# Dense expert stage: the next four experts' first activation is traced between the second and third block's values instead of in front of all five

## The chip, the cores and the metric

The kernel runs on one core of one Trainium2 chip. The metric is the device time of one execution in microseconds (us). Five engines of the core run instruction streams of their own: PE (matmuls), DVE (elementwise), ACT (activations and casts), POOL (here: it issues the indirect loads of single rows) and SP (it issues all other loads). Each engine takes its stream strictly in order; semaphores tie them together.

## The reference, cut to what matters

The reference is one layer of a streaming encoder over 1024 prompt and 128 sample tokens: attention and an RG-LRU, then a PEER layer, in which each token has 8 heads that choose 16 of 16384 one-neuron experts each. The change lies in the PEER layer:

```
act = jax.nn.gelu(jnp.einsum('thkd,td->thk', expert_u[e_idx], xt))
out = jnp.einsum('thk,thkd->td', g * act, expert_v[e_idx])
```

The 1152 tokens are nine blocks of 128. Four blocks (`GATHER`) load the rows of their experts one by one. The other five (`DENSE`, 640 tokens) are computed against all 16384 experts: with a matrix G of weights that is zero wherever a token has not chosen an expert, out = (G * gelu(U x)) V. The experts come as 128 groups of 128; the kernel calls such a group an expert, `e`.

## The kernel before

`dense` works through the 128 groups in 32 chunks of `ECH = 4`. In one chunk there are two kinds of work.

`u_phase(e, gt)`, once for each of four groups: load 512 KB of `peer_ut` into a `raw` buffer, split it into a high and a low part (`hi` on ACT, L141; `lo` on DVE, L142), and multiply in two halves of 320 tokens, 24 matmuls each (three products for each of 8 slices, L175 to L177), into two `pp` buffers in PSUM. ACT takes the gelu of each half into `wf` (L1043; this tile has a single buffer). DVE multiplies `wf` by that group's slice of `gt` (L1045), and the product is split into `wh` (ACT, L141) and `wl` (DVE, L142). The next group's gelu can't be written until `wl` has been read out of `wf`.

`v_phase(c, ws, vs)`, once for each chunk: for each of the five token blocks, in the order 2, 0, 3, 1, 4, it accumulates four groups times three products times two halves, so 24 matmuls of 512 columns (L1069), into an `S` buffer in PSUM. Blocks 0 and 1 keep buffers of their own over the whole stage. Blocks 2, 3 and 4 take turns in the one remaining buffer: each must be added into its `acc` by DVE (L1077) before the next may start.

`load_v(e)` loads 512 KB of `peer_v` into a `raw` buffer and splits it (`vh`, `vl`; four buffers each, free when the last block of a chunk has read them). The pool `raw` has four buffers, shared by the loads of both kinds. `load_g(c)` loads the four slices of G for a chunk (`gt`, 1280 KB, L1056) into a single buffer, so it can't be issued until the last group of the chunk before has been multiplied at L1045.

The loop before traces, for chunk c: `u_phase` and `load_v` of groups 1, 2, 3; `load_g` of the next chunk; `u_phase` of the next chunk's group 0; `v_phase`; `load_v` of the next chunk's group 0. The work of the five blocks therefore stands behind the first activation of the next chunk.

After the dense stage the code traces `gather` for the blocks 5, 6 and 7, and what the earlier stages have left of block 0: for each row a load issued by POOL into one of six buffers (L910, 512 KB) and a DVE instruction of 1.2 to 1.3 us (L937 for the dot products, L958 for the sums).

The order on each engine is not the order of the code. The program is built under `tile.TileContext(nc, schedule_with_timeline_sim=True)`: a planner lays out each engine's stream before the run, by the durations that it assumes. What is traced first has priority; what is traced later is put in where the planner sees an engine free and the operands ready. In this way DVE carries rows of the gather between the instructions of the dense stage, and PE takes matmuls of `v_phase` between those of `u_phase`. On the chip the streams are fixed: an instruction whose operand is late holds up everything behind it on its engine.

Of the kernel before, what the change touches and what calls it, by code (L numbers as in the profile page):

```python
# [58 lines left out]
ECH = 4  # L59
AT_ONCE = (0, 5)  # L60
LAG = 3
FLOW = ((0,) * 5, (0.2, 0.26, 0.26, 0.26, 0.26), (0.13, 0.26, 0.3, 0.26, 0.26))


def r32(ap):
    return ap.bitcast(F32R)
# [3 lines left out]
def kernel(ctx, tc, a):  # L70
# [49 lines left out]
    def rstd_of(ss, q_="", r=None):  # L120
        m = sm_p.tile([128, 1], F32, name="rs_m" + q_)
        V.tensor_scalar(m, ss, 1.0 / D, EPS, op0=ALU.mult, op1=ALU.add)
        if r is None:
            r = sm_p.tile([128, 1], F32, name="rs_r" + q_)
        S.activation(r, m, ACTF.Sqrt)
        V.reciprocal(r, r)
        q = sm_p.tile([128, 1], F32, name="rs_q" + q_)
        V.tensor_tensor(q, r, r, op=ALU.mult)
        V.tensor_tensor(q, q, m, op=ALU.mult)
        V.tensor_scalar(q, q, -0.5, 1.5, op0=ALU.mult, op1=ALU.add)  # L130
        V.tensor_tensor(r, r, q, op=ALU.mult)
        return r

    def ssq(x, junk, q_=""):
        ss = sm_p.tile([128, 1], F32, name="ss" + q_)
        S.activation(junk, x, ACTF.Square, accum_out=ss)  # L136
        return ss
# [13 lines left out]
    def load_split(src, hi=None, lo=None, shape=(128, KT, 128), raw=None, key=None):  # L151
        if raw is None:
            raw = w_p.tile(list(shape), F32, name="raw", tag="raw", bufs=RAW_BUFS)
            nc.sync.dma_start(raw, src)
        if hi is None and phase[0] in THIRD and nw[0] % 3 == 2:
            hi = g_p.tile(list(shape), F32, name="hi", tag="g3")
            lo = g_p.tile(list(shape), F32, name="lo", tag="g4")
        elif hi is None:
            hi = w_p.tile(list(shape), F32, name="hi", tag="hi")
            lo = w_p.tile(list(shape), F32, name="lo", tag="lo")  # L160
        nw[0] += 1
        if key in lo_d:
            S.copy(r32(hi), raw)  # L163
            nc.sync.dma_start(lo, lo_d[key])
            return hi, lo
        split(hi, lo, raw)
        if phase[0] == 0 and key:

            lo_d[key] = dr_p.tile(list(shape), F32, name="lo_%s%d" % key)
            nc.sync.dma_start(lo_d[key], lo)  # L170
        return hi, lo

    def mm3(out, l, r, first, last):
        (lh, ll), (rh, rl) = l, r
        T.matmul(out, r32(lh), r32(rh), start=first, stop=False)  # L175
        T.matmul(out, r32(lh), r32(rl), start=False, stop=False)  # L176
        T.matmul(out, r32(ll), r32(rh), start=False, stop=last)  # L177
# [9 lines left out]
    def transpose_in(x, dst, c0, ps_s=ps_s):  # L187

        pt = ps_s.tile([128, 8, 128], F32, name="tr", tag="S")
        for k in range(8):  # L190
            T.transpose(pt[:, k, :], x[:, k * 128:(k + 1) * 128], ident)
        split(dst[:, 0, :, c0:c0 + 128], dst[:, 1, :, c0:c0 + 128], pt)
# [13 lines left out]
    def tick(n=1):  # L206

        for _ in range(n):
            if fill:
                fill.popleft()()  # L210
# [37 lines left out]
    def mixer(mp, gi, t0, xn):  # L248
# [20 lines left out]
        def beat(us):  # L269
# [9 lines left out]
            if flow:  # L279
                due[1] += FLOW[gi][stage[0]] * us  # L280
                while due[1] >= 1.0:
# [618 lines left out]
    def finish(b, x2, tmp, nf=None, q_=""):  # L900
        r = rstd_of(ssq(x2, tmp, q_), q_)
        if nf is None:
            nf = tmp
            nc.sync.dma_start(nf, a["norm_final"].to_broadcast([128, D]))
        V.scalar_tensor_tensor(x2, x2, r, nf, op0=ALU.mult, op1=ALU.mult)  # L905
        nc.sync.dma_start(a["y"][b], x2)
# [7 lines left out]
    def gather(b):  # L914
# [7 lines left out]
        nc.sync.dma_start(xt, xt_d[b])  # L922
        lag = LAG if early else 0

# [93 lines left out]
    def dense(dp):  # L1018
        nd = len(DENSE)
        Td = nd * 128  # L1020
        xt2 = dp["x"].tile([128, 2, KT, Td], F32, name="xd")
        accs = [None, None]
        for i, b in enumerate(DENSE):
            x = (w_p.tile([128, D], F32, name="xt", tag="raw", bufs=RAW_BUFS) if i < RAW_BUFS else
                 w_p.tile([128, D], F32, name="xt", tag="lo"))
            nc.sync.dma_start(x, xt_d[b])
            transpose_in(x, xt2, i * 128, dp["ps"])

        ps_p = dp["pp"]
        ps_s = dp["ps"]  # L1030

        def u_phase(e, gt):
            tick(2)
            hi, lo = load_split(a["peer_ut"][e], raw=u0 if e == 0 else None)
            wh = dp["w"].tile([128, Td], F32, name="wh")
            wl = dp["w"].tile([128, Td], F32, name="wl")
            w = dp["w"].tile([128, Td], F32, name="wf", bufs=1)
            for m in range(0, Td, Td // 2):
                c1 = slice(m, m + Td // 2)
                ps = ps_p.tile([128, Td // 2], F32, name="pp", tag="pp")  # L1040
                for k in range(KT):
                    mm3(ps, (hi[:, k, :], lo[:, k, :]), (xt2[:, 0, k, c1], xt2[:, 1, k, c1]), k == 0, k == KT - 1)
                S.activation(w[:, c1], ps, ACTF.Gelu_apprx_tanh)  # L1043
            w3 = w.rearrange("p (c t) -> p c t", t=32)
            V.tensor_tensor(w3, w3, gt[:, :, e % ECH, :], op=ALU.mult)  # L1045
            split(wh, wl, w)
            return wh, wl

        def load_v(e):
            vh = dp["v"].tile([128, D], F32, name="vh")  # L1050
            vl = dp["v"].tile([128, D], F32, name="vl")
            return load_split(a["peer_v"][e], vh, vl, (128, D))

        def load_g(c):
            gt = dp["g"].tile([128, NCH, ECH, 32], F32, name="gt")
            nc.sync.dma_start(gt, G_d[:, :, c * ECH:(c + 1) * ECH, :].rearrange("n p i t -> p n i t"))  # L1056
            return gt

        kept = [ps_s.tile([128, 2, 512], F32, name="S", tag="S") for _ in range(2)]

        def v_phase(c, ws, vs, nf=None):
            for i in (2, 0, 3, 1, 4):
                held = i < len(kept)
                po = kept[i] if held else ps_s.tile([128, 2, 512], F32, name="S", tag="S")
                c1 = slice(i * 128, i * 128 + 128)
                for n, ((wh, wl), (vh, vl)) in enumerate(zip(ws, vs)):
                    for q, (l, r) in enumerate(((wh, vh), (wh, vl), (wl, vh))):
                        for m in range(2):
                            T.matmul(po[:, m, :], r32(l[:, c1]), r32(r[:, m * 512:m * 512 + 512]),  # L1069
                                     start=(n == 0 and q == 0 and (c == 0 or not held)),  # L1070
                                     stop=(n == ECH - 1 and q == 2 and (c == nch - 1 or not held)))
                if held and c == nch - 1:
                    acc = w_p.tile([128, D], F32, name="acc", tag="lo")
                    nc.sync.dma_start(acc, x2_d[DENSE[i]])
                    accs[i] = acc
                if not held or c == nch - 1:
                    V.tensor_tensor(accs[i], accs[i], po.rearrange("p m c -> p (m c)"), op=ALU.add)  # L1077
                if c == nch - 1:
                    finish(DENSE[i], accs[i], w_p.tile([128, D], F32, name="yo", tag="hi"), nf)

        nch = 128 // ECH
        gt = load_g(0)
        ws, vs = [u_phase(0, gt)], [load_v(0)]
        for i in range(2, nd):
            acc = dp["x"].tile([128, D], F32, name=f"acc{i}")
            nc.sync.dma_start(acc, x2_d[DENSE[i]])
            accs.append(acc)
        for c in range(nch):
            for e in range(c * ECH + 1, (c + 1) * ECH):
                ws.append(u_phase(e, gt))  # L1090
                vs.append(load_v(e))
            nxt = []
            if c + 1 < nch:
                gt = load_g(c + 1)
                nxt = [u_phase((c + 1) * ECH, gt)]
            nf = None
            if not nxt:
                nf = w_p.tile([128, D], F32, name="nf", tag="raw", bufs=RAW_BUFS)
                nc.sync.dma_start(nf, a["norm_final"].to_broadcast([128, D]))
            v_phase(c, ws, vs, nf)  # L1100
            ws = nxt
            vs = [load_v((c + 1) * ECH)] if nxt else []

    mp = {nm: es_m.enter_context(tc.tile_pool(name=nm, bufs=bufs, reuse_waits="tile"))
          for nm, bufs in (("big", 2), ("s", S_BUFS), ("kv", 2), ("b", 2), ("c", 4))}
# [39 lines left out]
    for n, blocks in enumerate(GROUPS):  # L1145
# [17 lines left out]
        for b in SELECT[n]:  # L1163
            if b in AT_ONCE:
                fill.extend(late_picks[b])
            else:
                _, rest, heads = select(b)
# [132 lines left out]
```

## Time and profile before

| what | us |
|---|---|
| time, median of three runs | 3982.32 (3981.56 to 3986.05) |
| the profiled execution | 3979.21 |
| its span, first to last instruction | 3977.3 |
| dense stage, first to last matmul of it | 2010.1 to 3966.5 |

The span is the time between the first and the last instruction in the trace. The profiled execution's own time lies 1.9 us above its span and 3.1 us below the median. All stretches below are in us from the start of the span.

### The profile page before, as it was taken

How to read it: one execution, taken by the hardware profiler on the slowest of the kernel's cores; microseconds unless marked ns; L12 is line 12 of the kernel's file. 1: busy time of each engine (PE TensorE's matmuls, PEld its weight loads, DVE VectorE, ACT ScalarE, POOL GpSimd, SP SyncE). 2: the span in 40 equal slices, each digit the busy share in tenths (PEclk: the TensorE clock that was granted, in tenths of full speed). 3: DMA queues.
4: the chain of work that ended last, by engine and by line, in shares of the span. 5: the costliest groups of instructions: out<-in, count | busy, mean ns of one | idle time of the engine just before them, and what ended most of it. 6: DMA issues, size and time to landing. Idle time of an engine off the chain costs nothing. (4 is left out here: it accounts for less than half of the span.)

```text
span 3977.3 us, 59539 instructions
## 1 busy us (share of the span) xinstructions
PE 3647.0 (92%) x21775; PEld 3264.7 (82%) x21775; DVE 3042.7 (77%) x6332; ACT 1618.2 (41%) x2699; POOL 1405.4 (35%) x1094
## 2 busy tenths in 40 slices
PE   8998899898998999888888889999999899999998
PEld 7877799876887987778888778888888888888887
DVE  8433357868675879987778888888877887877887
ACT  7554346556644845665532122222222222222222
POOL 0000000122221023222106555655664655655653
PEclk9999999999998999999999999999999999999999
DMA  7778887888899898879968888989888889888986
GB/s 260 253 243 317 296 283 271 327 308 269 316 385 331 294 346 292 292 281 360 379 203 308 306 287 296 320 314 343 311 305 293 322 313 332 311 304 305 331 311 233
DMA packets 470358, 1208.05 MB, mean 304 GB/s; under 512 B 41008, under 2 KB 199088, under 8 KB 467504
## 3 DMA queue, kind: packets, MB, share of 16 engines
q1 hardware_dynamic: 292496, 638.23, 45.2%
q0 software_dynamic: 147456, 536.94, 37.8%
q10 hardware_dynamic: 30112, 29.09, 2.1%
q8 instruction: 170, 2.79, 0.3%
q14 instruction: 124, 1.02, 0.1%
HBM read 1066.15 MB, written 137.94 MB: 303 GB/s over the span
## 5 line engine op out<-in xcount | busy, mean ns | idle before, releaser
L910 POOL DMA_INDIRECT row<-peer_u,ei x512 | 698.0, 1363 | 1260.5 <-DVE row L937 631.3
L910 POOL DMA_INDIRECT row<-peer_v,ei x512 | 683.3, 1334 | 828.7 <-DVE x L958 525.4
L958 DVE SCALAR_TENSOR_TENSOR x<-row,q,x 128x1024 f32<-128x1024 f32 x512 | 655.3, 1280 | 27.2 <-DMA row<-peer_v,ei 20.8
L175 PE MATMUL pp<-xd,hi 128*128 128x320 f32 x2048 | 639.8, 312 | 31.9 <-ACT wf L1043 26.9
L937 DVE SCALAR_TENSOR_TENSOR row<-row,xt 128x1024 f32<-128x1024 f32 x512 | 613.6, 1217 | 66.1 <-DMA row<-peer_u,ei 64.4
L176 PE MATMUL pp<-xd,hi 128*128 128x320 f32 x2048 | 637.5, 311 | 0.3 <-DVE xd L142 0.3
L177 PE MATMUL pp<-xd,lo 128*128 128x320 f32 x2048 | 636.8, 311 | 0.0
L175 PE MATMUL pp<-xn,hi 128*128 128x384 f32 x1344 | 477.4, 356 | 19.1 <-ACT st L1011 7.8
L1069 PE MATMUL S<-vh,wh 128*128 128x512 f32 x1280 | 410.0, 402 | 62.2 <-DVE acc L1077 54.0
L177 PE MATMUL pp<-xn,lo 128*128 128x384 f32 x1344 | 459.4, 343 | 2.1 <-DMA lo<-lo_w_in 2.1
L176 PE MATMUL pp<-xn,hi 128*128 128x384 f32 x1344 | 460.6, 343 | 0.1
L1069 PE MATMUL S<-vh,wl 128*128 128x512 f32 x1280 | 401.1, 402 | 27.6 <-DVE wl L142 27.6
L175 PEld LDWEIGHTS pp<-xd,hi 128*128 128x128 f32 x2048 | 389.9, 190 | 42.6 <-ACT wf L1043 30.7
L141 ACT CAST hi<-raw 128x1024 fp32r<-128x1024 f32 x223 | 233.8, 1049 | 429.0 <-PE pp L176 307.2
L1069 PE MATMUL S<-vl,wh 128*128 128x512 f32 x1280 | 404.0, 397 | 0.0
L176 PEld LDWEIGHTS pp<-xd,hi 128*128 128x128 f32 x2048 | 389.8, 190 | 7.2 <-DVE xd L142 0.6
L177 PEld LDWEIGHTS pp<-xd,lo 128*128 128x128 f32 x2048 | 389.2, 190 | 1.6
L142 DVE TENSOR_TENSOR lo<-raw,hi 128x1024 fp32r<-128x1024 f32 x223 | 271.9, 1220 | 150.1 <-ACT hi L141 134.8
L141 ACT CAST wh<-wf 128x640 fp32r<-128x640 f32 x128 | 93.3, 729 | 616.8 <-DVE wf L1045 583.6
L1069 PEld LDWEIGHTS S<-vh,wh 128*128 128x128 f32 x1280 | 239.3, 193 | 112.3 <-DVE acc L1077 60.9
L163 ACT CAST hi<-raw 128x1024 fp32r<-128x1024 f32 x192 | 200.4, 1047 | 296.5 <-PE pp L176 204.3
L1069 PEld LDWEIGHTS S<-vh,wl 128*128 128x128 f32 x1280 | 246.7, 194 | 84.6 <-DVE wl L142 32.7
(296 smaller groups left out, 6821.7 us busy)
## 6 DMA issues: line engine op xcount, KB each, us to landing
raw<-w_in SPq DMA_DIRECT2D x168, 512.0 KB
raw<-peer_v SPq DMA_DIRECT2D x128, 512.0 KB
raw<-peer_ut SPq DMA_DIRECT2D x127, 512.0 KB
lo<-lo_w_in SPq DMA_DIRECT2D x112, 512.0 KB
G_d<-st SPq DMA_DIRECT2D x20, 2048.0 KB
gt<-G_d SPq DMA_DIRECT2D x32, 1280.0 KB
lo_w_in<-lo SPq DMA_DIRECT2D x56, 512.0 KB
raw<-wq SPq DMA_DIRECT2D x48, 512.0 KB
```

Of the source, the lines that this page charges most:

```text
L141: S.copy(r32(hi), src)
L142: ins = V.tensor_tensor(r32(lo), src, hi, op=ALU.subtract)
L163: S.copy(r32(hi), raw)
L175: T.matmul(out, r32(lh), r32(rh), start=first, stop=False)
L176: T.matmul(out, r32(lh), r32(rl), start=False, stop=False)
L177: T.matmul(out, r32(ll), r32(rh), start=False, stop=last)
L910: P.indirect_dma_start(out=t, out_offset=None, in_=table, in_offset=bass.IndirectOffsetOnAxis(ap=ei[:, j:j + 1], axis=0))
L937: V.scalar_tensor_tensor(u, u, 1.0, xt, op0=ALU.mult, op1=ALU.mult, accum_out=hh[:, j:j + 1])
L958: V.scalar_tensor_tensor(x2, v, q[:, j:j + 1], x2, op0=ALU.mult, op1=ALU.add)
L1069: T.matmul(po[:, m, :], r32(l[:, c1]), r32(r[:, m * 512:m * 512 + 512]), start=(n == 0 and q == 0 and (c == 0 or not held)), stop=(n == EC ...
```

## The change

The first activation of the next chunk (`u_phase` of its group 0) is traced inside `v_phase`, behind its blocks 2 and 0 and ahead of 3, 1 and 4: `v_phase` becomes a generator that yields after each block, and `MIDST = {1: 1, 3: 0}` says how many activations are traced after the k-th block. The load of the next `gt` still stands ahead of `v_phase`. The rest of the next chunk follows behind block 4 in the order `load_v` 0, `load_v` 1, `u_phase` 1, `load_v` 2, `u_phase` 2, `load_v` 3, `u_phase` 3; before, each `u_phase` stood ahead of its own group's `load_v`. The number of instructions, their shapes and the sizes of all pools stay as they are. The first chunk's four activations are traced at once ahead of the loop, and the last chunk has no following one.

```diff
+MIDST = {1: 1, 3: 0}
...
         def v_phase(c, ws, vs, nf=None):
...
                     finish(DENSE[i], accs[i], w_p.tile([128, D], F32, name="yo", tag="hi"), nf)
+                yield
...
+        for e in range(1, ECH):
+            ws.append(u_phase(e, gt))
+            vs.append(load_v(e))
         for c in range(nch):
-            for e in range(c * ECH + 1, (c + 1) * ECH):
-                ws.append(u_phase(e, gt))
-                vs.append(load_v(e))
-            nxt = []
-            if c + 1 < nch:
+            more = c + 1 < nch
+            nf = None
+            if more:
                 gt = load_g(c + 1)
-                nxt = [u_phase((c + 1) * ECH, gt)]
-            nf = None
-            if not nxt:
+            else:
                 nf = w_p.tile([128, D], F32, name="nf", tag="raw", bufs=RAW_BUFS)
                 nc.sync.dma_start(nf, a["norm_final"].to_broadcast([128, D]))
-            v_phase(c, ws, vs, nf)
-            ws = nxt
-            vs = [load_v((c + 1) * ECH)] if nxt else []
+
+            nxt = []
+            for k, _ in enumerate(v_phase(c, ws, vs, nf)):
+                for _ in range(MIDST.get(k, 0) if more else 0):
+                    nxt.append(u_phase((c + 1) * ECH + len(nxt), gt))
+            ws, vs = nxt, []
+            if more:
+                left = ECH - len(ws)
+                for k in range(ECH):
+                    vs.append(load_v((c + 1) * ECH + k))
+                    while ECH - len(ws) > left - (left * (k + 1)) // ECH:
+                        ws.append(u_phase((c + 1) * ECH + len(ws), gt))
```

## Rows read from the trace of the kernel before

**Rows 1.** Stretches: length, busy us (instructions) by engine, granted clock, DMA share, GB/s.

```profile
2010.00:2527.00 517.00, 451.60 (x2441) 405.83 (x2440) 461.70 (x1095) 126.16 (x176) 257.31 (x182) 0.96 0.81 282
2527.00:3892.00 1365.00, 1309.29 (x7175) 1183.83 (x7174) 1119.05 (x1279) 336.53 (x472) 815.95 (x570) 0.98 0.88 315
```

**Rows 2.** Instructions on `gt`, 2500 to 3900: duration ns, first and last start.

```profile
L1056 SPq DMA_DIRECT2D gt<-G_d x24: 377/377/890, 2527.3 to 3892.4; - x24
```

**Rows 3.** PE in order of time, 3000 to 3021: start, us, instruction.

```profile
3000.00 0.31 PE L175 MATMUL pp<-xd,hi 128*128 128x320 f32 x1
...
3007.04 0.63 PE L1069 MATMUL S<-vh,wh 128*128 128x512 f32 x2
...
3014.68 0.63 PE L1069 MATMUL S<-vh,wh 128*128 128x512 f32 x2
...
3020.16 0.31 PE L176 MATMUL pp<-xd,hi 128*128 128x320 f32 x1
```

**Rows 4.** Waits of PE, 2527 to 3892: us in total, times, longest.

```profile
PE S L1069 <- DVE acc L1077: 44.3, 17, 6.7
PE S L1069 <- DVE wl L142: 9.9, 5, 3.9
```

**Rows 5.** Waits of PE, 2010 to 2527.

```profile
PE pp L175 <- ACT wf L1043: 26.7, 8, 7.7
PE S L1069 <- DVE wl L142: 17.7, 7, 4.2
```

**Rows 6.** Waits of DVE, 2527 to 3892.

```profile
DVE wf L1045 <- DMA gt<-G_d: 159.7, 22, 9.2
DVE row L937 <- DMA row<-peer_u,ei: 33.5, 36, 4.3
```

**Rows 7.** SP in order of time, 3054 to 3125.

```profile
3060.49 0.38 SPq L1056 DMA_DIRECT2D gt<-G_d  x1
```

**Rows 8.** DVE in order of time, 3054 to 3125; in brackets its idle time.

```profile
3059.64 0.82 DVE L1045 TENSOR_TENSOR wf<-wf,gt 128x640 f32<-128x640 f32 x1
...
3061.57 0.82 DVE L142 TENSOR_TENSOR wl<-wf,wh 128x640 fp32r<-128x640 f32 x1
...
3068.41 1.28 DVE L958 SCALAR_TENSOR_TENSOR x<-row,q,x 128x1024 f32<-128x1024 f32 x1
3078.84 0.82 DVE L1045 TENSOR_TENSOR wf<-wf,gt 128x640 f32<-128x640 f32 x1 [9.15 <-DMA gt<-G_d]
...
3081.52 6.56 DVE L958 SCALAR_TENSOR_TENSOR x<-row,q,x 128x1024 f32<-128x1024 f32 x5
3088.00 1.21 DVE L1077 TENSOR_TENSOR acc<-acc,S 128x1024 f32<-128x1024 f32 x1
```

**Rows 9.** ACT in order of time, 3060 to 3064.5.

```profile
3064.03 0.42 ACT L1043 ACTIVATE wf<-pp 128x320 f32<-128x320 f32 x1
```

**Rows 10.** PE in order of time, 3052 to 3097.

```profile
3054.82 0.31 PE L175 MATMUL pp<-xd,hi 128*128 128x320 f32 x1
...
3076.97 0.31 PE L177 MATMUL pp<-xd,lo 128*128 128x320 f32 x1
...
3089.27 1.22 PE L1069 MATMUL S<-vh,wh 128*128 128x512 f32 x2 [6.71 <-DVE acc L1077]
```

**Rows 11.** The stretch just behind that wait.

```profile
3089.20:3096.90 7.70, 7.63 (x24) 6.10 (x25) 7.59 (x8) 3.15 (x3) 5.76 (x5) 0.71 0.95 341
```

**Rows 12.** DMA queues, 3061 to 3078.5: packets, MB, share of 16 engines.

```profile
q0 software_dynamic: 1122, 4.06, 60.8%
q1 hardware_dynamic: 2841, 2.29, 41.7%
```

**Rows 13.** The chain of work that ended last, 3690 to 3730.

```profile
3690.28 7.81 DMA raw<-peer_ut
...
3708.92 18.47 DMA gt<-G_d
```

**Rows 14.** Instructions on `x`, 3700 to the end.

```profile
L958 DVE SCALAR_TENSOR_TENSOR x<-row,q,x x107: 1267/1285/1331, 3699.0 to 3942.0; 128x1024 f32<-128x1024 f32 x107
```

## The prediction

> **What bounds the kernel now.** I read the stretches first: in the body of the dense stage, 2527 to 3892, PE is busy for 1309 of 1365 us, DVE for 1119, and the DMA engines for 88% [rows 1]. That looks like a kernel at PE's limit, but the matmuls overlap in the records, so I priced PE by the distance between starts. One activation (48 matmuls) takes 7.04 us, 0.147 each; 24 matmuls of `v_phase` take 5.48 us, 0.228 each [rows 3]. A chunk has 192 of the first and 120 of the second: 28.2 + 27.4 = 55.6 us if PE never waits. The loads of `gt`, one for each chunk, give what a chunk takes: 24 issues from 2527.3 to 3892.4 are 23 chunks of 59.35 us [rows 2]. So PE loses 3.8 us in each, 87 us in this body. The eight chunks before it take 517 us [rows 1], about 64.6 each, and lose more.
>
> The view of waits tells who ends the loss. In the body it is nearly all PE's wait for `acc` at L1077, 44.3 us in 17 waits [rows 4]: a block's values can't start because the buffer of the one before hasn't been added. In the first eight chunks it is the gelu (26.7 us) and `wl` (17.7 us) [rows 5]. DVE is not slow at adding; it stands. Its own longest wait is for `gt` at L1045, 159.7 us in 22 waits, 7.3 each [rows 6].
>
> One chunk in order of time shows the link. SP issues the load of `gt` at 3060.49 [rows 7], just behind the last product of the old one at 3059.64 [rows 8]. The new chunk's first activation starts on PE at 3054.82 [rows 10], its second gelu is done at 3064.45 [rows 9], and DVE comes to the product at 3069.69 (3068.41 + 1.28). But `gt` lands 18.35 us after its issue: the product starts at 3078.84 after 9.15 us of standing. Behind it in DVE's stream are `wl`, five rows of the gather and the `acc` of block 3, at 3088.00 [rows 8]. PE, which had run ahead with 37 matmuls of the next activation since 3076.97, waits 6.71 us for that `acc` until 3089.27 [rows 10]. The clock comes on top: in the next 7.7 us the granted clock is 0.71 of 2.4 GHz on average, a mixture of its two levels, and the 24 matmuls take 7.63 us instead of 5.48 [rows 11, 3]. That is 2.15 us more after 6.71 us of waiting, or 0.32 for each us waited.
>
> **The change part by part.** No instruction is added or removed. PE's work stays 55.6 us a chunk, and DVE's and ACT's stay too. What moves is one activation (48 matmuls, two gelus, three splits and a product) with its load, behind the rest of blocks 2 and 0; and the later loads of V go one place ahead of the activations.
>
> The load of `gt` doesn't start earlier: it still needs the last product of the chunk before. What moves is its first use. PE goes from the fourth activation to blocks 2 and 0 and then to the new activation. If all 48 matmuls of these two blocks are still to do, that is 48 x 0.228 = 10.96 us later, and the gelu is done 3.96 + 10.96 = 14.9 us after the load's issue, against 18.35 for the landing: DVE stands for 3.4 us instead of 9.15. If half of them have been done early, as PE's interleaved stream does now, the shift is 5.5 us, and DVE stands for up to 8.9 us, as now. What counts for PE is the other end of the wait. From the end of the fourth activation, 3054.82, to the landing are 24.0 us; the product, one row, `wl` and `acc` add 0.82 + 1.28 + 0.82 + 1.21 = 4.1 [rows 8], so `acc` of block 3 is done 28.1 us after the fourth activation. PE's work until block 4 wants it is blocks 2 and 0 (10.96), the new activation (7.04), block 3 (5.48) and block 1 (5.48): 29.0 us. It is just covered. With half of blocks 2, 0 and 1 done early it is 5.48 + 7.04 + 5.48 + 2.74 = 20.7, and PE waits 7.4.
>
> Which of the two comes is decided by whether the activations 1, 2 and 3 run one behind the other. They do if the steps from an activation's last matmul to its `wl` take no longer than the next activation's 7.04 us. In the trace they took 7.6 us (3054.82 to 3062.39 [rows 8]), with a `lo` split and a row of the gather ahead of `wl` on DVE. Now one activation is drawn forward into the gap ahead of block 4, and the rest meet DVE when it splits the four V loads. In the new order all three follow block 4 evenly. I take it that they nearly run through, so most of the 48 matmuls remain, and that four fifths of the body's `acc` waits go: 44.3 x 1.32 = 58.5 us with the clock, of which 46.8 are saved (bounds 0 and 58.5). In the first eight chunks I take half of the gelu waits, which also come of the late `wl` behind `gt`: 26.7 x 1.32 = 35.2, of which 17.6 (bounds 0 and 35.2).
>
> The moved activation was also cover. Block 2 follows the fourth activation, and needs its `wl`, 7.6 us later. Before, the 7.04 us of the new activation lay in between. Now there are the first three groups' matmuls of blocks 2 and 0, 36 x 0.228 = 8.2 us, if they are all still to do; otherwise the planner can still put the new activation in, by priority. The waits for `wl` are 9.9 us in 23 chunks now [rows 4], 0.43 each. I add as much again, 31 x 0.43 = 13.3 us (bounds 0, and 7.6 - 2.74 = 4.9 a chunk, 151 us, if half is done early and nothing is put in).
>
> The loads: four V loads wait in the four `raw` buffers until block 4 reads the old ones out, so the fourth activation's load is issued some 4 us into block 4 (its first group's 1.4, a cast, a split). It needs 7.8 us to land [rows 13] and some 2.5 for its split, 14.3 in all, and PE wants it after block 4 and two activations, 5.5 + 14.1 = 19.6 us. The 5 us of slack hide it; I charge 3 us in all (bounds 0, and 2 us a chunk, 62, if it landed 7 us later).
>
> Sum: -46.8 - 17.6 + 13.3 + 3 = -48.1 us. Against the profiled execution, 3979.2 (span 3977.3), that is 3931.1. The median of the runs is 3.1 above it: 3934.
>
> The Trainium skill ("DMA: Bandwidth & Descriptors", section "Queues, rings and completion order") states that each DMA engine takes turns between the queues that have work, packet by packet. In the stretch of the `gt` load the trace agrees in kind: the row loads of the gather moved 4.06 MB in 1122 packets and SP's queue 2.29 MB in 2841 smaller ones [rows 12]. By that rule the load stays long for as long as rows are being loaded, wherever its use stands, and a gather that DVE no longer holds up would make it longer. By it alone the wait would go on as the first rival has it, at 3982.
>
> **The rivals.** *The wait stays where it is.* The planner keeps a third or more of the blocks' matmuls early, DVE still reaches the product some 10 us after the issue, and PE still waits at block 4. For it: the stream now does so, and 7.6 us is more than 7.04. Savings and new `wl` waits cancel: 3982, within 8.
>
> *Slower: block 4 loses its filler.* The 37 matmuls that now stand between block 3 and block 4 come after block 4. If half of blocks 2, 0 and 1 was done early, PE waits 24.0 + 4.1 - 20.7 = 7.4 us in a chunk like the one shown, or 5.5 with the mean 7.3 instead of 9.15 us of standing. In all 23 chunks of the body that is 127 us instead of 44.3: 83 x 1.32 = 110 us, 4092; in half of them 55 us, 4037, which I take as its time. It decides when fewer than some 48 of the 72 matmuls of blocks 2, 0 and 1 remain behind the fourth activation. Against it: the even order of the activations.
>
> *The gather becomes the end.* Its last row is at 3942.0 [rows 14], 24.5 us ahead of the last matmul. If PE gains 48 us but DVE's stream is laid out such that the rows come later, only some 24 us plus a little show: 3955. Against it: rows stand behind the same `gt` and come forward with it; DVE is busy for 48.7 of 59.35 us in a chunk (1119 / 23), and stands 33.5 us in the body for rows that haven't landed [rows 6], so there is room.
>
> *Everything goes well.* All `acc` and gelu waits of these kinds go and none is added: 58.5 + 35.2 = 93.7, 3889; with the `wl` waits too (27.6 x 1.32 = 36.4), 3852.
>
> **How the numbers follow.** My sum has 0.48, with a range of its own from 3890 to 3962; the wait stays 0.15; slower 0.24; the gather as the end 0.10; the best case 0.03. About 0.2%, 8 us, is what a measurement of this kernel can tell from no change. Faster is 0.48 + 0.10 + 0.03 = 0.61, same 0.15, slower 0.24. The predicted time is 3934. The range goes from 3880, below the saving of all named waits, to 4015, where about half of the slower case lies outside: some 0.05 below and 0.14 above.
>
> **What would show it.** Right: DVE's wait for `gt` falls from 159.7 us in the body to below some 70; PE's wait for `acc` to about 10; the `gt` issues come some 57.5 us apart; the granted clock of the body rises; between the fourth activation and the next one PE shows some 40 to 48 matmuls of `v_phase`. Wrong: `acc` waits of 5 to 7 us in most chunks straight behind blocks 3 and 1, with no activation between (the lost filler); waits for `wl` of several us at block 2 in each chunk (the lost cover); waits for `raw` ahead of the fourth activation's split; or rows of the gather behind the last block. The forecast falls if the blocks' matmuls are still done early, for the cover is then short by 7 us a chunk.

## The result and the profile after

The changed kernel takes 4022.86 us (median of four runs, 4017.26 to 4027.07) against 3981.94 for the kernel before (four runs, 3976.21 to 3986.05): a ratio of 1.0094, interval 1.0069 to 1.0119. It is slower, by 41 us, and above the range that I gave.

First the lengths, in the page of the changed kernel (the span) and in the views of a line and of a tile (the dense stage's weight loads and the issues of `gt`: shortest, median and longest duration in ns, first and last start).

```profile
span 4025.1 us, 59558 instructions
```

```profile
L176 PEld LDWEIGHTS pp<-xd,hi x2048: 186/188/334, 2026.1 to 3991.6; 128*128 128x128 f32 x187
...
L1057 SPq DMA_DIRECT2D gt<-G_d x24: 377/377/870, 2560.1 to 3935.6; - x24
```

The lengths follow by subtraction. From the first dense matmul to the first of these issues it is 534.0 us, where it was 517.2 (2010.1 to 2527.3 [rows 2]); the next 23 chunks take 1375.5 instead of 1365.1, 59.80 each instead of 59.35; the rest takes 89.5 instead of 84.9. So 31.8 us are lost from the start of the dense stage on, over half of them, 16.8, in its first eight chunks. Another 16.0 lie ahead of it: it starts at 2026.1 instead of 2010.1. Together these are the 47.8 us between the two spans. That is 7 more than the 41 between the medians, because the profiled execution is 2.7 us below the median of its kernel before and 4.2 above it after.

Stretches of the changed kernel, with the columns of rows 1:

```profile
2026.00:2560.00 534.00, 459.92 (x2434) 410.68 (x2433) 468.75 (x1100) 126.95 (x176) 257.93 (x187) 0.94 0.81 278
2560.00:3936.00 1376.00, 1306.58 (x7170) 1182.46 (x7169) 1121.10 (x1281) 340.01 (x473) 814.06 (x571) 0.98 0.88 313
```

PE's and DVE's work in the body is what it was [rows 1]. What grew is waiting. PE's waits in the first stretch, then PE's and DVE's in the body (in total, times, longest); between them PE's wait for `acc` in the first stretch of the kernel before, which rows 5 leave out:

```profile
PE S L1071 <- DVE acc L1079: 18.4, 4, 7.0
PE pp L176 <- ACT wf L1044: 16.3, 3, 6.6
PE S L1071 <- DVE wl L143: 11.0, 4, 3.9
PE S L1071 <- DVE vl L143: 9.2, 4, 4.7
PE S L1071 <- ACT wh L142: 8.6, 4, 3.0
PE pp L176 <- ACT hi L142: 7.9, 4, 3.9
```

```profile
PE S L1069 <- DVE acc L1077: 8.8, 5, 3.5
```

```profile
PE S L1071 <- DVE acc L1079: 49.7, 19, 7.1
PE S L1071 <- DVE wl L143: 18.9, 8, 3.8
...
DVE wf L1046 <- DMA gt<-G_d: 143.5, 21, 10.0
```

DVE stands for `gt` 6.8 us in each chunk instead of 7.3 (143.5 / 21 against 159.7 / 22 [rows 6]). The `acc` wait that was to go is still there, 49.7 us instead of 44.3 [rows 4]. The `wl` wait nearly doubled. In the first stretch the gelu wait fell by 10.4 us [rows 5], but the `acc` wait, 8.8 us there before, is 18.4, and a wait for `vl` is new.

One chunk in order of time, the one behind that of rows 7 to 10. First the kernel before (SP's issue, DVE's product, PE's wait), then SP, DVE and PE of the changed kernel, and the stretch behind PE's wait.

```profile
3123.18 0.38 SPq L1056 DMA_DIRECT2D gt<-G_d  x1
...
3141.15 0.83 DVE L1045 TENSOR_TENSOR wf<-wf,gt 128x640 f32<-128x640 f32 x1 [8.20 <-DMA gt<-G_d]
...
3150.25 0.73 PE L1069 MATMUL S<-vh,wh 128*128 128x512 f32 x2 [3.58 <-DVE acc L1077]
```

```profile
3159.25 0.38 SPq L1057 DMA_DIRECT2D gt<-G_d  x1
```

```profile
3158.40 0.82 DVE L1046 TENSOR_TENSOR wf<-wf,gt 128x640 f32<-128x640 f32 x1
...
3170.24 1.23 DVE L143 TENSOR_TENSOR lo<-raw,hi 128x1024 fp32r<-128x1024 f32 x1 [0.16 <-ACT hi L142]
...
3178.62 0.82 DVE L1046 TENSOR_TENSOR wf<-wf,gt 128x640 f32<-128x640 f32 x1 [7.16 <-DMA gt<-G_d]
3179.37 1.28 DVE L959 SCALAR_TENSOR_TENSOR x<-row,q,x 128x1024 f32<-128x1024 f32 x1
3180.56 0.82 DVE L143 TENSOR_TENSOR wl<-wf,wh 128x640 fp32r<-128x640 f32 x1
3181.30 2.60 DVE L959 SCALAR_TENSOR_TENSOR x<-row,q,x 128x1024 f32<-128x1024 f32 x2
3183.81 1.22 DVE L1079 TENSOR_TENSOR acc<-acc,S 128x1024 f32<-128x1024 f32 x1
```

```profile
3185.08 1.22 PE L1071 MATMUL S<-vh,wh 128*128 128x512 f32 x2 [3.80 <-DVE acc L1079]
```

```profile
3185.00:3192.70 7.70, 7.62 (x22) 6.08 (x23) 7.59 (x8) 2.77 (x3) 5.77 (x5) 0.64 0.84 251
```

`gt` lands 19.4 us after its issue (3159.25 to 3178.62), where it was 18.0 (3123.18 to 3141.15). DVE comes to the product at 3171.47, 12.2 us after the issue; before, it was 9.8. The product moved, but by 2.4 us, and as the median of 21 chunks of the body by 1.2 (from 11.1 to 12.2). Behind it, still, stand `wl`, three rows of the gather and the `acc` of block 3, and PE waits for that `acc` ahead of block 4, 3.80 us instead of 3.58. After it the granted clock is again a mixture of its two levels, 0.64 on average.

The order of PE's own work in that chunk, counted from the trace, behind the fourth activation (v: matmuls of the blocks, n: the new activation, f: the activation after it):

```
before: n24 v5 n24 v33 f6, block 3, f30, block 4
after:  v14 n31 v12 n17 v9, block 3, v7 f20, block 4
```

Before, 38 matmuls of blocks 2, 0 and 1 were left behind the fourth activation; now 42 are. And 26 of them, not 48, stand ahead of the last matmul of the new activation.

In the first eight chunks the order turned round. In the third to the seventh, 4 or 5 matmuls of these blocks were done ahead of the fourth activation's end before the change, and 46 to 50 (19 in the last of them) came between it and the new activation's end; after the change, 48 are done early in each of the five, and 4 to 6 come between. In two of these chunks the waiting product now stands ahead even of block 2's `acc`, and PE waits 2.7 and 6.2 us for that one ahead of block 3.

### The profile page after: what moved, and what is told of

Its sections match the earlier page's. It is cut to its first block, busy times and chain, and to the rows that moved or that the text cites. A ratio compares the mean times of both kernels' runs of the same rounds, so it can differ in the third digit from the quotient of the medians.

```text
span 4025.1 us, 59558 instructions
## 1 busy us (share of the span) xinstructions
PE 3668.8 (91%) x21775; PEld 3282.8 (82%) x21775; DVE 3044.4 (76%) x6332; ACT 1623.9 (40%) x2699; POOL 1396.9 (35%) x1094
## 5 line engine op out<-in xcount | busy, mean ns | idle before, releaser
L1071 PEld LDWEIGHTS S<-vl,wh 128*128 128x128 f32 x1280 | 247.2, 193 | 64.9 <-DVE vl L143 10.9
```

## The experiments

Each was timed in five rounds beside the kernel before. Two questions: which half of the change costs the time, and whether the late `gt` is the way in which it does.

**One half at a time.** The first kernel keeps the moved activation and puts each U phase ahead of its own V load again. Against the changed kernel:

```diff
-                left = ECH - len(ws)
-                for k in range(ECH):
-                    vs.append(load_v((c + 1) * ECH + k))
-                    while ECH - len(ws) > left - (left * (k + 1)) // ECH:
-                        ws.append(u_phase((c + 1) * ECH + len(ws), gt))
+                vs.append(load_v((c + 1) * ECH))
+                for e in range((c + 1) * ECH + 1, (c + 2) * ECH):
+                    ws.append(u_phase(e, gt))
+                    vs.append(load_v(e))
```

> The moved activation alone: it stands between the second and third block as in the change, but each later activation is again traced ahead of its own V load. If the change loses by the moved activation (block 2 loses its cover, DVE still stands for gt): 30 to 45 us above the kernel before, waits of PE for wl in the body near 19 us and for acc near 50. If it loses by the order of the loads: within 10 us of the kernel before, and the waits for the V split and for the U split that are new in the first eight chunks (9 and 8 us) are gone.

Measured: 4008.29 against 3978.32, 1.0073 (1.0053 to 1.0093). That is 30 us, the lower bound of the first forecast, but the `wl` waits of its body are 11.4 us, not 19. The second kernel keeps the new order of the loads and puts the activation in front of all five blocks again:

```diff
-            for k, _ in enumerate(v_phase(c, ws, vs, nf)):
-                for _ in range(MIDST.get(k, 0) if more else 0):
-                    nxt.append(u_phase((c + 1) * ECH + len(nxt), gt))
+            if more:
+                nxt.append(u_phase((c + 1) * ECH, gt))
+            for _ in v_phase(c, ws, vs, nf):
+                pass
```

> The order of the loads alone: the first activation stands in front of all five blocks as before, but the V loads go one place ahead of the activations, as in the change. If the loss is in the moved activation: within 8 us of the kernel before. If it is in the order of the loads: 25 to 45 us above it. If both: 10 to 25, and the two single edits add up to the 41 us of the change.

Measured: 4009.20 against 3978.32, 1.0075 (1.0057 to 1.0092), 31 us; the two don't add up as the last forecast has it. PE's longest-summed wait in the body of each, first the moved activation alone (2565 to 3960), then the loads alone (2571 to 3954):

```profile
PE S L1071 <- DVE acc L1079: 74.7, 22, 7.5
```

```profile
PE S L1071 <- DVE acc L1079: 57.5, 19, 6.4
```

Each half alone costs about 30 us, and the two together 41, not 60. The `acc` wait is there in both: 74.7 us with the moved activation alone, in an execution 21 us above the median of its kernel, and 57.5 with the loads alone, which is no clear step from 44.3 and 53.8 in two profiles of the kernel before. So neither half holds the cause alone; both change the stream that the planner lays out around the same wait.

**Take the late operand away, in both orders.** These two kernels load `gt` once, for the first chunk, and leave the other 31 loads of it out, so that all chunks multiply by the first chunk's weights. The order around it is that of before in the first, which loses the line `gt = load_g(c + 1)`, and that of the change in the second:

```diff
-            if more:
-                gt = load_g(c + 1)
-            else:
+            if not more:
```

> The order before, but G is loaded for the first chunk alone and that tile is used for all 32 (31 loads of gt are left out, so the dense blocks' values are not the reference's). If the late gt causes PE's waits for acc and for the gelu, as the prediction has it: 70 to 100 us below the kernel before, the waits for acc in the body near zero. If those waits come from DVE's own load of rows and splits: not more than 25 us below.

> The changed order, with G loaded once in the same way (31 loads left out). If what the change loses comes only with the late gt: within 8 us of the same edit on the kernel before. If it comes from the lost cover and the loads: 20 to 40 us above that.

Measured: 3871.62 for the old order, 0.9733 (0.9714 to 0.9751), and 3866.34 for the new, 0.9724 (0.9703 to 0.9744). PE's waits and the stretch (columns as in rows 1), for the old order and then for the new:

```profile
PE S L1069 <- DVE acc L1077: 1.3, 1, 1.3
```

```profile
2495.00:3788.00 1293.00, 1283.87 (x7182) 1170.06 (x7182) 1143.89 (x1303) 341.05 (x477) 824.51 (x581) 1.00 0.88 315
```

```profile
PE S L1071 <- DVE wl L143: 3.8, 2, 2.9
PE S L1071 <- ACT wh L142: 3.3, 2, 2.0
PE S L1071 <- DVE acc L1079: 1.5, 1, 1.5
```

```profile
2503.00:3791.00 1288.00, 1279.47 (x7176) 1166.87 (x7175) 1136.73 (x1297) 343.52 (x477) 797.14 (x575) 1.00 0.88 314
```

The two orders tie. Without the late `gt`, the activation as lost cover costs nothing in the body: the `wl` wait of the new order is 3.8 us in 1288, and 3.7 in the old one. The new place of the loads still shows in the first eight chunks, where PE waits 8.4 us for `vl` instead of 2.5, but the gelu wait there is 0.4 instead of 9.8, so that on balance nothing is lost. The place of the product does not cost by itself either: in the new order with `gt` loaded once it stands between the `acc` of blocks 2 and 3 in all 21 chunks counted, as in the changed kernel. So what the change costs in the dense stage hangs on the late `gt`. (The planner lays out other streams when the loads are missing; these are two kernels compared, not one instruction moved.) And the whole wait, with the transfer that makes it, was worth 107 us in the kernel before, above the 70 to 100 that I expected of this run, and between the two values that I gave for the best case (94 and 130).

**Move only the waiting instruction.** In the old order, the new activation's product and its splits are traced behind the `acc` of block 3, and tied behind it in DVE's stream (`issue_after`), so that `acc` can't stand behind `gt`:

```diff
-            w3 = w.rearrange("p (c t) -> p c t", t=32)
-            V.tensor_tensor(w3, w3, gt[:, :, e % ECH, :], op=ALU.mult)
-            split(wh, wl, w)
+            def fin():
+                w3 = w.rearrange("p (c t) -> p c t", t=32)
+                V.tensor_tensor(w3, w3, gt[:, :, e % ECH, :], op=ALU.mult)
+                split(wh, wl, w)
...
-                    V.tensor_tensor(accs[i], accs[i], po.rearrange("p m c -> p (m c)"), op=ALU.add)
+                    ins = V.tensor_tensor(accs[i], accs[i], po.rearrange("p m c -> p (m c)"), op=ALU.add)
+                    if i == 3 and fin is not None:
+                        with tc.issue_after(ins.ins):
+                            fin()
...
```

> The order before, but the moved group's product with gt and its two splits are tied behind block 3's acc on DVE; its matmuls and gelus stay in front of all five blocks. If PE's wait at block 4 is only that this acc stands behind the product in DVE's stream: waits for acc in the body fall from 44 us to under 10, and the time by 35 to 60 us. If the wait only moves on to the next gelu or to the V splits: within 10 us of the kernel before.

Measured: 3915.30 against 3979.46, 0.9842 (0.9815 to 0.9868). The waits of its body (2547 to 3849):

```profile
PE S L1073 <- DVE wl L142: 5.7, 3, 2.7
...
PE S L1073 <- DVE acc L1081: 0.6, 2, 0.3
...
DVE wf L1046 <- DMA gt<-G_d: 46.6, 13, 7.0
```

Every load is still made. DVE still waits for `gt` in 13 chunks, but PE no longer waits for `acc`, and the gain, 64 us, is a little more than the 35 to 60 expected: what stands behind the product now isn't wanted yet. The tie also brings DVE to the product later, 20.7 us after the issue of `gt` as the median of 21 chunks instead of 11.1, so that its wait for `gt` fell too. The runs don't part the two effects, except in those 13 chunks.

**Make the load shorter.** `gt` in two halves of two groups each, in two buffers, so that the first half can be issued two groups earlier, in the old order and in the new:

```diff
-            gt = dp["g"].tile([128, NCH, ECH, 32], F32, name="gt")
-            nc.sync.dma_start(gt, G_d[:, :, c * ECH:(c + 1) * ECH, :].rearrange("n p i t -> p n i t"))
-            return gt
+            gts = []
+            for h in range(2):
+                gt = dp["g"].tile([128, NCH, 2, 32], F32, name="gt")
+                e0 = c * ECH + 2 * h
+                nc.sync.dma_start(gt, G_d[:, :, e0:e0 + 2, :].rearrange("n p i t -> p n i t"))
+                gts.append(gt)
+            return gts
...
```

> The order before, with gt loaded as two halves of two groups each, in two buffers of half the size (the same memory; runs of 256 instead of 512 bytes): the first half can be loaded once the second group's product is done. If the late landing is the cause: DVE's wait for gt under 40 us in the body, 50 to 90 us below the kernel before. If twice the number of packets costs as much as it gives: within 20 us either way.

> The changed order with the same two halves. If the change loses by the cover of block 2 and the order of the loads: still 20 to 40 us above the halves in the order before. If it loses by where DVE stands for gt: within 10 us of them.

Measured: 3930.13, 0.9878 (0.9856 to 0.9899), and 3932.52, 0.9883 (0.9860 to 0.9905). Again the orders tie, with the product ahead of block 3's `acc` in all 21 chunks of both: it does no harm there when `gt` has landed. 49 us is just short of what was forecast. Two stretches of the first: the body, and the end behind the last block.

```profile
2486.00:3762.00 1276.00, 1276.00 (x7175) 1165.41 (x7174) 1047.83 (x1222) 337.54 (x472) 734.74 (x513) 1.00 0.92 313
...
3830.00:3941.00 111.00, 0.00 (x0) 0.00 (x0) 94.13 (x93) 2.28 (x6) 73.77 (x62) 0.50 0.89 331
```

PE never stands in the body. But then the gather is the end: in the last 111 us of this execution (13 us above its kernel's median) PE does nothing and DVE works off 93 instructions. That is my third rival, in a kernel that gains 49 us, as much as the change was to gain.

**Both kernels again.**

> The changed kernel once more, for its spread: the streams up to the dense stage are the same as before, but in the first profile the dense stage began 16 us later. If that is chance of single executions: the dense stage of this profile begins within 5 us of 2010 to 2020 in a quicker execution, and the median lies at 4015 to 4025. If it belongs to the change: again at 2023 or later.

> The kernel before once more, for the stretch ahead of the dense stage, whose streams no version changes. If the 16 us that the changed kernel's profile lost there are chance of single executions: the dense stage of this profile may begin anywhere between 2003 and 2026, and its length stays at 1967 within 8 us. If they belong to the change: again 2010 within 3 us.

Measured: the changed kernel 4016.47 against 3979.46, 1.0092 (1.0068 to 1.0116); the kernel before 3984.59 against 3982.93, 1.0000 (0.9985 to 1.0015). The first weight load of the dense stage and PE's `acc` wait in the body, changed kernel, then before:

```profile
L176 PEld LDWEIGHTS pp<-xd,hi x2048: 186/188/334, 2025.9 to 3990.6; 128*128 128x128 f32 x187
```

```profile
PE S L1071 <- DVE acc L1079: 57.2, 20, 7.9
```

```profile
L175 PEld LDWEIGHTS pp<-xd,hi x2048: 186/188/331, 2013.2 to 3953.4; 128*128 128x128 f32 x187
```

```profile
PE S L1069 <- DVE acc L1077: 53.8, 18, 6.3
```

The later start of the dense stage is there again, 12.7 us. The `acc` wait of one kernel differs between its profiles by up to 9.5 us (44.3 and 53.8), so the step from 44.3 to 49.7 is no growth that can be told; that the wait did not go is.

**The tie in the changed order, and other places of the activation.** The tied kernel is the changed one with the same `fin` as above for the moved activation. The next two move the activation behind the fourth block (`MIDST = {1: 0, 3: 1}`) and behind the third (`{2: 1, 3: 0}`):

```diff
-                    nxt.append(u_phase((c + 1) * ECH + len(nxt), gt))
+                    nxt.append(u_phase((c + 1) * ECH + len(nxt), gt, True))
...
+                    if i == 3 and fins:
+                        with tc.issue_after(ins.ins):
+                            fins.pop()()
```

> The changed order, with the moved group's product and its splits tied behind block 3's acc on DVE. If the change loses only because that acc stands behind a product that waits for gt: within 10 us of the same tie on the order before (0.984 of the kernel before). If the lost cover of block 2 or the order of the loads costs by itself: 20 to 40 us above it.

> The changed kernel with one constant different: the activation stands behind the fourth block (2, 0, 3, 1) instead of behind the second. In its laid-out DVE stream the product then stands behind block 3's acc in 16 of 21 chunks looked at, in the changed kernel in none. If that order is the cause: 25 to 60 us below the kernel before. If moving the activation back costs by the cover that it takes from block 2: at or above the changed kernel's 4020.

> The changed kernel with the activation behind the third block (2, 0, 3), one block later than in the change and one earlier than the version that gained. In its laid-out DVE stream the product still stands ahead of block 3's acc in 19 of 21 chunks, as in the changed kernel. If that order decides: still 20 to 45 us above the kernel before, as the changed kernel. If each block of delay helps by itself: midway between behind the second (+37) and behind the fourth (-46), so within 15 us of the kernel before.

Measured: tied 3903.81 against 3982.93, 0.9811 (0.9793 to 0.9830), the fastest of all that leave nothing out, 12 us below the same tie in the old order, though the two intervals overlap; behind the fourth block 3936.68, 0.9886 (0.9867 to 0.9905); behind the third 4001.32 against 3979.02, 1.0058 (1.0037 to 1.0079). The tied kernel's waits in the body, then DVE in order of time in one chunk:

```profile
PE S L1078 <- DVE acc L1086: 7.6, 2, 4.0
PE S L1078 <- DVE wl L143: 4.1, 3, 2.0
...
DVE wf L1049 <- DMA gt<-G_d: 43.2, 14, 8.7
```

```profile
3048.59 1.22 DVE L1086 TENSOR_TENSOR acc<-acc,S 128x1024 f32<-128x1024 f32 x1
...
3055.34 0.82 DVE L1049 TENSOR_TENSOR wf<-wf,gt 128x640 f32<-128x640 f32 x1 [5.53 <-DMA gt<-G_d]
...
3066.50 1.21 DVE L1086 TENSOR_TENSOR acc<-acc,S 128x1024 f32<-128x1024 f32 x1
```

DVE stands 5.53 us for `gt` here too. It costs PE nothing, because block 3's `acc` at 3048.59 is already done and the next, block 4's, is wanted a block later. The waits with the activation behind the fourth block, then behind the third:

```profile
PE S L1071 <- DVE wl L143: 9.2, 4, 3.5
PE S L1071 <- DVE acc L1079: 7.8, 4, 3.1
...
DVE wf L1046 <- DMA gt<-G_d: 36.2, 13, 8.1
```

```profile
PE S L1071 <- DVE acc L1079: 61.2, 18, 6.7
...
DVE wf L1046 <- DMA gt<-G_d: 153.8, 21, 9.2
```

I counted in DVE's streams where the waiting product stands, over 21 chunks of the body. Ahead of block 3's `acc`: all 21 before (in one of them ahead of block 2's too), 21 after the change, 21 in each of the two kernels with half of the change, 19 with the activation behind the third block. Behind it: 21 in both tied kernels, 16 with the activation behind the fourth block. Every kernel of the first list has 44 to 75 us of `acc` wait in the body and none of them gains; every one of the second has under 8 and gains 46 to 79 us.

## Why the prediction was wrong

**What bound the kernel: right.** The chain late `gt`, product, `acc`, PE is what held PE up. Taking `gt` away gave 107 us and a granted clock of 1.00 in the body; moving the product and its splits behind the `acc` brought the old order 64 us and the new one 79 us below the kernel before.

**The failed step** is the one I named as the decision: "I take it that they nearly run through, so most of the 48 matmuls remain". They don't. As the median of 21 chunks, 33 of the 72 matmuls of blocks 2, 0 and 1 were done early before the change, and 30 are after it: 42 remain, where I needed 48. Of those only 25 come ahead of the new activation's end. The planner again put the activation in early, in pieces between the blocks' matmuls. Being traced behind two blocks lowered its priority; it didn't fix its place. So DVE came to the product 1.2 us later as the median (2.4 in the chunk shown), not 11, and after 12.2 us still met a load that takes 18 to 19.

From there the balance at block 4 follows. In the chunk shown, `acc` was done 28.9 us after the fourth activation's last matmul (3156.12, where the next matmul starts, to 3185.03; I had 28.1), and PE had, from the counts above, 14 + 12 + 9 + 24 + 7 = 66 matmuls of the blocks and 31 + 17 + 20 = 68 of activations: 66 x 0.228 + 68 x 0.147 = 25.0 us of work. It was short by 3.9, and waited 3.80. The rule of balance holds in this chunk; what I put into it didn't. That 28.9 is so near 28.1 is luck. The landing came 22.5 us behind the fourth activation instead of 24.0, and from there to the end of `acc` it was 6.4 us instead of 4.1. I had counted one row of the gather on this way, where the chunk of rows 8 has six and takes 10.4 us; the median of the body is 7.7 us before and 6.1 after.

**Term by term**, in us of waiting of the profiled execution, times 1.32 as in the prediction. `acc` in the body: -46.8 predicted, +7.1 measured (5.4 x 1.32), within what two profiles of one kernel differ. Gelu in the first eight chunks: -17.6 predicted, -13.7 measured (10.4), the one saving that came. `wl` in the body: +13.3 predicted, +11.9 measured (9.0), right in size by luck, for it comes of the late `gt` and not of the lost cover that I gave as its reason. Loads: +3 predicted; the new wait for `vl` in the first chunks is 9.2, so +12.1. Not in my sum: `acc` in the first chunks, +12.7 (9.6). What is left in those chunks (`wl` 17.7 to 11.0, `hi` 3.9 to 7.9, `wh` 6.7 to 8.6) comes to -1.1. The measured terms add up to 29.0, against the 31.8 us by which the dense stage grew. The second pair of profiles (*Both kernels again*) gives, in the same order, +4.5, -10.3, +8.3, +12.4, +9.5 and +3.8, in sum 28.2 against 27.0. Of these 27.0, 17.4 lie in the first eight chunks and 5.3 in the body; where I had put a saving of 17.6, most of the loss arose.

**The rivals.** The time came near the rival *block 4 loses its filler* (4037), but not by its detail: the filler isn't lost. Between block 3 and block 4 PE has 20 and 7 matmuls in the chunk shown, and as a median 5.3 us of work against 5.0 before. *The wait stays where it is* describes the body best (10 us more in 1365, and 5 in the second pair). *The gather becomes the end* did not come here, but in the kernels with halves. I had the lost cover as a cost of its own; with `gt` in time it costs nothing, so the `wl` waits too are an effect of a DVE that stands.

By the Trainium skill ("DMA: Bandwidth & Descriptors", section "Queues, rings and completion order"), which the prediction cites, each DMA engine takes turns, packet by packet, between the queues that have work. By that rule the load of `gt` stays long as long as rows are being loaded, wherever its use stands. The traces agree in kind. These rows of the view of `gt` give the shortest, median and longest landing in the body of the kernel before (its second profile), of the changed kernel (the same) and of the tied kernel, whose DMA queues move more in the body, 330 GB/s instead of 313:

```profile
DMA to landing us min/median/max: 8.7/18.2/20.3
...
DMA to landing us min/median/max: 8.3/18.4/20.5
...
DMA to landing us min/median/max: 10.6/19.7/24.9
```

No run here takes the row loads away, so that they are what makes the load long is not shown. I cited the rule for the first rival and gave it nothing in the sum. It spoke for moving the use a long way, and the change moved it 1.2 us.

**Open.** Of the difference of the spans, 16.0 of 47.8 us in one pair of profiles and 12.7 of 39.7 in the other lie ahead of the first changed instruction. Up to the start of the dense stage all five engines carry the same instructions, on DVE, POOL and SP in the same order too; it still comes at 2026.1 and 2025.9 in the changed kernel and at 2010.1 and 2013.2 before. It isn't the order as such: with `gt` loaded once the dense stage starts at 2003.3 in the old order and 2005.5 in the new, and with the old order and halves at 2024.1. Each program seems to have its own value, and no run here says why. Open, too, is why each half of the change alone costs 30 us (7 to 10 of them again lie ahead of the dense stage, which starts at 2020.1 and 2019.8); the runs show only that they don't add up and that the changed order costs nothing once `gt` isn't late.

## What to carry to other kernels

Where a planner lays out the streams, moving the code of an instruction moves its priority; whether the instruction itself moves has to be forced or bounded, and the shift to count on is that of the stream, not that of the text. For a late operand on an in-order engine, ask what stands behind the waiting instruction and who needs it: here a tie behind the `acc` that PE wanted brought the old order 64 us and the changed one 79 us below the kernel before, while a change that shortened DVE's wait by half a microsecond left PE's wait where it was. And when that wait is gone, look at once for what ends next, as the gather did with 111 us.

## What the runs showed of the hardware

The granted clock is the second price of short waits: it was 0.64 over the 7.7 us behind a wait of 3.80 us, and 1.00 over the whole body in the three kernels shown whose PE hardly waited, against 0.98 before and after the change, with 54 and 69 us of `acc` and `wl` waits in it. The median landing of the same 1280 KB load in the body was 18.2 us before and 19.7 in the tied kernel, with single loads between 8.7 and 24.9. With `gt` in halves the DMA engines were busy for 92% of the body instead of 88%, and PE still never waited.
